# The last K part of a down projection in three column groups, with the final norm beside it

## The chip, the core and the metric

The kernel runs on one core of a Trainium2 chip. The metric is the device time of one execution in microseconds (us). TensorE (PE in the profile) multiplies; VectorE (DVE), ScalarE (ACT) and GpSimd (POOL) work on the elements; SyncE (SP), ACT and POOL start DMA transfers. Each engine runs its own instructions in the order in which they stand, and semaphores hold an instruction until what it needs is there.

## What is computed

A decoder layer over 528 positions (16 meta tokens and 512 tokens) of width 1024. Only its end matters here: a gated MLP whose down projection is added to the residual `h`, and a final RMSNorm over the 1024 channels.

```python
hn = rmsnorm(h, norm2_g[l])
up = causal_dwconv(hn @ w_up[l], conv_w[l], conv_b[l])
a, bv = jnp.split(up, 2, axis=-1)
h = h + (jax.nn.silu(a) * bv) @ w_down[l]      # K = 2816, N = 1024
return rmsnorm(h, final_norm_g)[:, N_META:]    # over the 1024 channels of each token
```

## The kernel before, in words

Channels lie on the 128 partitions and tokens along the free axis, so an activation of 1024 channels is 8 chunks of 128 x 528. Two neighbouring chunks share a tile: `h2.pair(i)` holds chunks 2i and 2i+1. All products are made to nearly full fp32 precision from rounded operands (type `F32R`): weights and activations are each split into a high and a low part (`split`, L270 to L272: ACT copies to the high part, DVE subtracts for the low one), and three products, high by high, high by low and low by high, are added up in PSUM. A matmul whose operands are plain `F32` is one instruction in the program and two records in the profile.

The tail of the program is a list `seq` of jobs (22 jobs "up", and the down projection in between and behind). The down projection's K of 22 blocks of 128 is cut into `PARTS` of 6, 6, 6 and 4 blocks; each part goes over the 8 output chunks in 4 jobs of two chunks (`c` = 0, 1). Part 0 and 1 stand among the "up" jobs, part 2 behind them, and part 3, the last four jobs (`base` = `len(seq) - 4`), has its own code, which is where the change is. `down` (L970 to L978) makes the products of one output chunk with one part: per block of K three matmuls against 128 x 128 weights, so 12 in part 3.

Part 3 before (L1003 to L1039): chunks 0 to 6 are each made over all 512 tokens at once (12 matmuls of 512 columns), DVE adds the sum to `h` (L1014), ACT squares it (L1019) and multiplies `h` by the norm's gain (`gf`, L1021), and the squares are added up in `tot3`, on POOL for four chunks and on DVE for two (L1020). Chunk 7 is made in two halves of 256 tokens. For each half, `ones32` (all ones, plain `F32`) times `tot3` and times the last chunk's squares gives the sum over the 1024 channels on every partition (L1026 and L1030), `rsqrt_mean` turns it into 1/root (ACT: Ln, L254, and Exp, L256; DVE: three steps that sharpen it, L258 to L260), and four multiplications of two chunks each (three on DVE, one on POOL, L1038) are followed by four output DMAs (L1039).

Weights of a down job arrive in a tile of the pool `rawp` (3 buffers, `fetch`, L574 for these jobs) over SP's queue and are split into two tiles of `gp` (2 buffers for high, 2 for low). So the split for a job waits until the products of the job two before it are done. The pool `ssp` (2 buffers of 1024 columns for high, 2 for low) holds block sums for the "up" jobs and is unused in parts 2 and 3. PSUM has 8 banks of 512 columns (`bank`), taken in turn.

The tile framework orders instructions of each engine when it builds the program. What ends up in which order is shown below where it matters.

Of the kernel before, what the change touches and what calls it, by code (L numbers as in the profile page):

```python
# [14 lines left out]
AF = mybir.ActivationFunctionType  # L15
ALU = mybir.AluOpType

P = 128
L = 528
META = 16  # L20
T0 = 14
TW = L - T0
D = 1024
# [17 lines left out]
CROSS = {(0, 1): 0, (1, 0): 1, (1, 1): 2, (2, 0): 3}  # L41
CROSS_X = {(0, 0): 0, (0, 1): 1, (1, 0): 2, (1, 1): 3}
PARTS = ((0, 6), (6, 6), (12, 6), (18, 4))
SUPERS = [(0, 16)] + [(16 + 128 * i, 128) for i in range(4)]

VEC = {}
# [26 lines left out]
def f32(ap):  # L73
    return ap.bitcast(F32)
# [3 lines left out]
def hybrid_block(ctx: ExitStack, tc: tile.TileContext, xt, g1d, wts, wsq, wdown, wglr, wgk, vecs, out):  # L78
    nc = tc.nc
    act, dve, pool, pe, sp = nc.scalar, nc.vector, nc.gpsimd, nc.tensor, nc.sync  # L80
# [46 lines left out]
    def big(name, dt=F32, home=None):  # L127
        return Pairs(name, home or HOME.get(name, firstp), dt)
# [4 lines left out]
    def ps(name):  # L133
        return psum.tile([P, 2, 512], F32, tag="ps", name=name)
# [42 lines left out]
    def project(name, j, xh, xl, cols, hook=None, ahead=PREP_AHEAD):  # L177
        hi, lo = chunk(j, ahead)
        acc = ps(name)
        products(acc, [(hi[:, k], lo[:, k], xh[k], xl[k]) for k in range(KT)], cols, hook=hook)  # L180
        return acc
# [13 lines left out]
    def parts_of(acc, cols):  # L195
        for s, (a, b) in enumerate(cols):
            yield (acc[s] if isinstance(acc, list) else acc[:, s])[:, : b - a], slice(a, b)
# [10 lines left out]
    def v1(name, i=0):  # L208
        c = VEC[name] + i
        return vec[:, c : c + 1]  # L210
# [16 lines left out]
    ones32 = const.tile([P, P], F32, tag="ones32", name="ones32")  # L227
# [24 lines left out]
    def rsqrt_mean(dst, acc, cols, n, tmp):  # L252
        for src, c in parts_of(acc, cols):
            act.activation(dst[:, c], src, AF.Ln, scale=1.0 / n, bias=eps_t)  # L254
        c = slice(cols[0][0], cols[-1][1])
        done = act.activation(dst[:, c], dst[:, c], AF.Exp, scale=-0.5)  # L256
        for src, h in parts_of(acc, cols):
            dve.scalar_tensor_tensor(tmp[:, h], src, n * EPS, dst[:, h], ALU.add, ALU.mult)  # L258
        dve.scalar_tensor_tensor(tmp[:, c], tmp[:, c], -0.5 / n, dst[:, c], ALU.mult, ALU.mult)
        last = dve.scalar_tensor_tensor(dst[:, c], tmp[:, c], 1.5, dst[:, c], ALU.add, ALU.mult)  # L260
        return done, last
# [8 lines left out]
    def split(hi, lo, src):  # L270
        act.activation(hi, src, AF.Copy)  # L271
        dve.tensor_tensor(lo, src, f32(hi), ALU.subtract)  # L272
# [11 lines left out]
    def scaled(dst, acc, cols):  # L284
# [9 lines left out]
        out=tri, in_=ones32, pattern=[[1, P]], base=0, channel_multiplier=-1,  # L294
# [32 lines left out]
    with tc.issue_after(ready[0].ins), tc.issue_after(ready[1].ins):  # L327
        for m in range(3):
            scaled(qk[4 + m], accs[m], FULL)
        acc = project("pk3", ORDER["k"] + 3, xh, xl, FULL)  # L330
# [7 lines left out]
    acc = ps("pglr")  # L338
# [35 lines left out]
    for i in range(2):  # L374
        two = slice(2 * i, 2 * i + 2)
# [12 lines left out]
    def head_decay(h):  # L388
# [3 lines left out]
        act.activation(q_far[:, T0:], b[:, T0:], AF.Exp, scale=-1.0 / TAU)  # L392
        for s, (t, n) in enumerate(SUPERS):
            if s:
# [12 lines left out]
    for m in range(8):  # L407
        acc = project(f"pv{m}", ORDER["v"] + m, xh, xl, FULL)
# [18 lines left out]
    def span(s):  # L427
        t, n = SUPERS[s]
        c = max(t, T0)
        return t, c, t + n - c  # L430
# [80 lines left out]
    for s in range(4):  # L511
        gla_back(s)
        gla_front(s + 1)
        hl = squares(s)
# [3 lines left out]
    hl = squares(4)  # L518
# [27 lines left out]
    def bank(name):  # L546
        return bankp.tile([P, 512], F32, tag="bank", name=name)

    between = {9: (0, 0), 10: (0, 2), 15: (1, 0), 16: (1, 2)}
    seq = [("plain", "u", 0)] + [("plain", "a", i) for i in range(3)]  # L550
# [5 lines left out]
    for i in range(FF):  # L556
        seq.append(("plain" if i < PLAIN else "fast", "up", i))
        if i in between:
            part, m = between[i]
            seq += [("down", part, m), ("down", part, m + 1)]  # L560
    seq += [("down", part, m) for part in (2, 3) for m in range(4)]
    loaded, own, sums = {}, {}, {}

    def fetch(n):
        if n >= len(seq) or n in loaded:
            return
        job = seq[n]
        t = rawp.tile([P, 4, 512], F32, tag="raw", name=f"raw{n}")
        if job[0] != "down":
            sp.dma_start(t, wsq[UNIT[job[1]] + job[2]])  # L570
        else:
            nk = PARTS[job[1]][1]
            flat_t = t.rearrange("p a b -> p (a b)")
            sp.dma_start(flat_t[:, 0 : 2 * nk * P], wdown[4 * job[1] + job[2], :, 0 : 2 * nk * P])  # L574
        loaded[n] = t

    def blocks(t):
        return t.rearrange("p a (k n) -> p a k n", n=P)
# [3 lines left out]
    def direct_tiles(n):  # L582
        if n not in own:
            fetch(n)
            job = seq[n]
            hl = [gp.tile([P, 3, 512], F32R, tag=f"g{c}", name=f"g{c}{n}") for c in "hl"]
            if job[0] == "down":
                k = 2 * PARTS[job[1]][1] * P
                hl = [t.rearrange("p a b -> p (a b)")[:, 0:k] for t in hl]
                own[n] = [t.rearrange("p (c k n) -> p c k n", c=2, n=P) for t in hl], hl, k  # L590
            else:
                own[n] = [blocks(t) for t in hl], hl, None
        return own[n]

    def split_here(n):
        return seq[n][0] == "down" or seq[n][1] in ("grp", "b", "o")
# [11 lines left out]
    def make_high(n):  # L608
        if n >= len(seq) or n in high_made:
            return  # L610
        high_made.add(n)
        _, (hi, lo), k = direct_tiles(n)
        if k is None:
            act.activation(hi, loaded[n][:, 0:3], AF.Copy)  # L614
            if split_here(n):
                dve.tensor_tensor(lo, loaded[n][:, 0:3], f32(hi), ALU.subtract)
        else:
            split(hi, lo, loaded[n].rearrange("p a b -> p (a b)")[:, 0:k])

    def two(name):  # L620
        return tuple(ssp.tile([P, 2, 4, P], F32R, tag=f"s{c}", name=f"s{c}_{name}") for c in "hl")
# [16 lines left out]
    def weights(n):  # L638
        make_low(n)
        make_high(n)  # L640
        make_sums(n)
        return (own[n][0], *sums.get(n, ()))
# [7 lines left out]
    def prepare(n, ins=None):  # L650
        fetch(n + 2)
        fetch(n + 3)
        behind(ins, make_low, n + 2)
# [4 lines left out]
    def pairtile(name, dt=F32):  # L658
        return flat(name, unitp, dt)
# [210 lines left out]
    for n in range(len(seq)):  # L870
        kind, name, i = seq[n]
# [16 lines left out]
        elif name == "ga":  # L888
            z, _ = unit_gate(n, i, name)
# [8 lines left out]
        elif name == "b":  # L898
            plain(n, i, pbh, pbl, TAIL, take_b)
            if i == 3:  # L900
                h2, h2h, h2l = big("h2", F32, unitp), big("h2h", F32R, lastp), big("h2l", F32R, lastp)
# [68 lines left out]
    def down(acc, w, c, part, cols):  # L970
        a, b = cols
        k0, nk = PARTS[part]
        for k in range(nk):
            for e, (p, q) in enumerate(((0, 0), (0, 1), (1, 0))):
                pe.matmul(  # L975
                    acc, w[p][:, c, k], gated[k0 + k][q][:, a:b],
                    start=k == 0 and e == 0, stop=k == nk - 1 and e == 2,
                )  # L978

    for n, job in enumerate(seq):  # L980
        if job[0] != "down" and job[1] != "up":
            continue
        if job[0] != "down":
            i = job[2]
# [7 lines left out]
        elif job[1] < 3:  # L992
# [3 lines left out]
            for c in range(2):  # L996
                acc = bank(f"pd{n}_{c}")
                down(acc, w, c, job[1], (0, 512))
                h = h2[2 * job[2] + c][:, META:]
                dve.tensor_tensor(h, acc, h, ALU.add)  # L1000
            prepare(n)

    sq3 = pairtile("sq3")  # L1003
    tot3, last3 = sq3[:, 0:512], sq3[:, 512:1024]
    base = len(seq) - 4
    for m in range(7):
        (w,) = weights(base + m // 2)
        make_high(base + m // 2 + 1)
        if m % 2:
            prepare(base + m // 2)  # L1010
        acc = bank(f"pe{m}")
        down(acc, w, m % 2, 3, (0, 512))
        h = h2[m][:, META:]
        dve.tensor_tensor(h, acc, h, ALU.add)  # L1014
        if m == 0:
            act.activation(tot3, h, AF.Square)
        else:
            sq = pairtile(f"n3_sq{m}")[:, 0:512]
            act.activation(sq, h, AF.Square)  # L1019
            (pool if m < 5 else dve).tensor_tensor(tot3, tot3, sq, ALU.add)  # L1020
        act.activation(h, h, AF.Copy, scale=v1("gf", m))  # L1021
    (w,) = weights(base + 3)
    for a, b in ((0, 256), (256, 512)):
        acc, s3 = bank(f"pd7_{a}"), bank(f"n3s_{a}")
        down(acc[:, 0:256], w, 1, 3, (a, b))
        pe.matmul(s3[:, 0:256], ones32, tot3[:, a:b], start=True, stop=False)  # L1026
        t = h2[7][:, META + a : META + b]
        dve.tensor_tensor(t, acc[:, 0:256], t, ALU.add)
        act.activation(last3[:, a:b], t, AF.Square)
        pe.matmul(s3[:, 0:256], ones32, last3[:, a:b], start=False, stop=True)  # L1030
        r3 = pairtile(f"r3_{a}")
        rstd3 = r3[:, 0:256]
        rsqrt_mean(rstd3, [s3], ((0, 256),), D, r3[:, 512:768])
        dve.tensor_scalar(t, t, v1("gf", 7), None, ALU.mult)
        wide = rstd3.unsqueeze(1).to_broadcast([P, 2, 256])
        for eng, q, i in ((dve, sp, 1), (pool, act, 0), (dve, sp, 2), (dve, act, 3)):
            y = h2.pair(i)[:, :, META + a : META + b]
            eng.tensor_tensor(y, y, wide, ALU.mult)  # L1038
            q.dma_start(out[2 * i : 2 * i + 2, :, a:b].rearrange("m p t -> p m t"), y)  # L1039


# [79 lines left out]
```

## Time and profile before

| | us |
|---|---|
| three runs, median (lowest to highest) | 833.92 (832.73 to 834.35) |
| the profiled execution | 836.4 |
| its span, from the first to the last instruction | 834.7 |
| chain that ended last: share of PE / DMA / DVE / ACT | 85% / 6% / 3% / 3% |
| first product of part 3 begins, from the span's start | 797.61 |
| last product of part 3 begins | 821.63 |

A run is timed without the profiler; the profiled execution is one more, 2.5 us above the median of the three. In the profile a row of the timeline has: start, time from the first record's start to the last one's end, engine, line, operation, tiles written and read, shape, and how many records were merged into the row. PEld is TensorE's loading of weights, which lies beside the products; PEclk is the clock that was granted to TensorE.

### The profile page before, as it was taken

What the parts mean: (1) busy time and instruction counts of PE and PEld (TensorE: products, weight loads), DVE (VectorE), ACT (ScalarE), POOL (GpSimd) and SP (SyncE); (2) the same over time, 40 slices, a digit from 0 to 9 for tenths busy, and PEclk for the clock granted to TensorE, in tenths of its full rate; (3) what the DMA queues carried; (4) which work ended last, traced back from release to release, by engine and by line L of the source; (5) the groups of instructions that cost most, each with busy time, mean ns of one, the idle gap of its engine ahead of it and who ended that gap; (6) DMA issues with size and microseconds to landing.
All of it is one profiled execution on the core that took longest, in us unless ns stands there. A gap on an engine that the chain in (4) does not pass through costs nothing.

```text
span 834.7 us, 14943 instructions
## 1 busy us (share of the span) xinstructions
PE 813.1 (97%) x6219; PEld 783.2 (94%) x6219; DVE 593.8 (71%) x887; ACT 477.9 (57%) x679; POOL 128.9 (15%) x153
## 2 busy tenths in 40 slices
PE   8999999999999999999999999999999999999994
PEld 6999999999999999999999999999989988999883
DVE  6668346779756797755564597998759965899845
ACT  7287244576655676644234457774557734786542
POOL 4000000011222122110003322220122110320021
PEclk9999999999999999999999999999999999999998
DMA  6413320158667778734342756875557644775102
GB/s 218 157 57 99 99 76 27 51 147 254 164 130 171 176 177 177 192 88 152 112 150 99 171 122 149 180 150 158 146 140 163 159 113 152 168 166 134 54 23 101
DMA packets 35572, 113.16 MB, mean 136 GB/s; under 512 B 3920, under 2 KB 6736, under 8 KB 29488
## 3 DMA queue, kind: packets, MB, share of 16 engines
q1 hardware_dynamic: 17856, 81.26, 29.4%
q0 software_dynamic: 16416, 29.89, 22.1%
q8 instruction: 48, 0.79, 0.4%
q10 hardware_dynamic: 1232, 1.05, 0.4%
q14 instruction: 20, 0.16, 0.1%
HBM read 110.10 MB, written 2.10 MB: 134 GB/s over the span
## 4 chain that ended last, share of the span: by engine, by line
PE 85%; DMA 6%; DVE 3%; ACT 3%; issue 1%; POOL 1%; SPq 0%; DVEq 0%; ACTq 0%
PE pp L672 18%; PE x L706 14%; PE pd L975 12%; PE q L706 9%; PE pv L172 6%; DMA gl<-in_wsq_dram 5%; PE y L706 5%; PE v L706 5%; PE pr L172 4%; PE pq L172 3%; PE pe L975 2%; PE pk L172 2%; PE pgrp L834 1%; PE po L472 1%; ACT gl L604 1%
## 5 line engine op out<-in xcount | busy, mean ns | idle before, releaser
L606 POOL DMA_DIRECT2D gl<-in_wsq_dram x114 | 102.0, 1207 | 500.3 <-ACT gl L604 421.9
L614 ACT ACTIVATE gh<-raw 128x1536 fp32r<-128x1536 f32 x47 | 69.9, 1486 | 61.0 <-PE pp L672 26.7
L633 DVE TENSOR_TENSOR raw<-raw 128x512 f32<-128x512 f32 x116 | 79.9, 689 | 26.7 <-ACT gh L614 14.3
L975 PE MATMUL pd<-g,gh 128*128 128x512 f32 (+1 forms) x304 | 93.3, 389 | 0.0
L975 PEld LDWEIGHTS pd<-g,gh 128*128 128x128 f32 x304 | 56.5, 188 | 12.3
L604 ACT ACTIVATE gl<-raw 128x1536 fp32r<-128x1536 f32 x38 | 56.2, 1478 | 9.3 <-issue 4.4
L975 PE MATMUL pd<-g,gl 128*128 128x512 f32 (+1 forms) x152 | 59.0, 388 | 0.0
L155 ACT ACTIVATE whi<-wraw 128x1024 fp32r<-128x1024 f32 (+2 forms) x28 | 25.9, 933 | 53.3 <-PE pv L172 25.8
L156 DVE TENSOR_TENSOR wlo<-wraw,whi 128x1024 fp32r<-128x1024 f32 (+2 forms) x28 | 30.6, 1100 | 7.0 <-ACT whi L155 5.8
L975 PEld LDWEIGHTS pd<-g,gl 128*128 128x128 f32 x152 | 28.6, 188 | 6.1
L960 ACT ACTIVATE cv<-z,vec 128x512 f32<-128x512 f32 x44 | 33.9, 813 | 0.0
L1000 DVE TENSOR_TENSOR h<-pd,h 128x512 f32<-128x512 f32 x24 | 16.5, 689 | 24.4 <-PE pd L975 24.3
L961 DVE SCALAR_TENSOR_TENSOR cv<-z,vec,cv 128x512 f32<-128x512 f32 x44 | 32.2, 746 | 0.0
L962 DVE SCALAR_TENSOR_TENSOR cv<-z,vec,cv 128x512 f32<-128x512 f32 x44 | 32.2, 746 | 0.0
L272 DVE TENSOR_TENSOR gl<-raw,gh 128x1536 fp32r<-128x1536 f32 (+1 forms) x16 | 26.0, 1624 | 6.4 <-ACT gh L271 6.4
L271 ACT ACTIVATE gh<-raw 128x1536 fp32r<-128x1536 f32 (+1 forms) x16 | 22.0, 1377 | 11.8 <-PE pd L975 9.1
L172 PE MATMUL pv<-xh,whi 128*128 128x264 f32 x128 | 26.4, 287 | 0.0
L172 PE MATMUL pr<-xh,whi 128*128 128x258 f32 (+1 forms) x128 | 25.9, 284 | 0.0
L172 PE MATMUL pv<-xl,whi 128*128 128x264 f32 x128 | 25.9, 283 | 0.0
L172 PE MATMUL pv<-xh,wlo 128*128 128x264 f32 x128 | 25.9, 283 | 0.0
L172 PE MATMUL pr<-xh,wlo 128*128 128x258 f32 (+1 forms) x128 | 25.8, 284 | 0.0
L172 PE MATMUL pr<-xl,whi 128*128 128x258 f32 (+1 forms) x128 | 25.6, 281 | 0.0
(1280 smaller groups left out, 2949.6 us busy)
## 6 DMA issues: line engine op xcount, KB each, us to landing
raw<-in_wsq_dram SPq DMA_DIRECT2D x47, 1024.0 KB, 5.7
gl<-in_wsq_dram POOLq DMA_DIRECT2D x114, 256.0 KB, 7.3
wraw<-in_wts_dram SPq DMA_DIRECT2D x22, 512.0 KB, 3.6
raw<-in_wdown_dram SPq DMA_DIRECT2D x12, 768.0 KB, 4.3
xb<-in_xt_dram SPq DMA_DIRECT2D x4, 528.0 KB, 5.4
h<-in_xt_dram SPq DMA_DIRECT2D x4, 514.0 KB, 5.3
raw<-in_wdown_dram SPq DMA_DIRECT2D x4, 512.0 KB, 3.5
x<-in_xt_dram SPq DMA_DIRECT2D x7, 264.0 KB, 6.2
```

The source lines that it names most:

```text
L156: dve.tensor_tensor(lo[:, a:b], t[:, a:b], f32(hi[:, a:b]), ALU.subtract)
L172: pe.matmul(acc[:, s, : b - a], w, x[:, a:b], start=(i == 0 and w is wh and x is xh), stop=(i == n - 1 and last),)
L604: act.activation(lo, loaded[n][:, 0:3], AF.Copy, scale=-1.0)
L606: pool.dma_start(lo[:, b], wsq[UNIT[name] + i, :, b], accum_op=ALU.add)
L614: act.activation(hi, loaded[n][:, 0:3], AF.Copy)
L633: dve.tensor_tensor(raw[:, dst], raw[:, dst], raw[:, x], ALU.add)
L672: pe.matmul(acc[:, 0 : b - a], w[p], q[k][:, a:b], start=k == 0 and e == 0, stop=k == KT - 1 and e == 2,)
L706: pe.matmul(acc[:, 0:n], w[a][:, block, k], x[k][b][:, at], start=first and k == 0 and e == 0, stop=k == 3 and e == 2, skip_group_check=no ...
L960: act.activation(cv, z[:, c, META:], AF.Identity, scale=v1("cw2", m), bias=v1("cb", m))
L961: dve.scalar_tensor_tensor(cv, z[:, c, META - 1 : L - 1], v1("cw1", m), cv, ALU.mult, ALU.add)
L962: dve.scalar_tensor_tensor(cv, z[:, c, META - 2 : L - 2], v1("cw0", m), cv, ALU.mult, ALU.add)
L975: pe.matmul(acc, w[p][:, c, k], gated[k0 + k][q][:, a:b], start=k == 0 and e == 0, stop=k == nk - 1 and e == 2,)
```

## The change

Part 3 goes over the tokens in three groups, `CUTS` of 224, 160 and 128 columns, and within each group over all four pairs of output chunks. So the weights of all four jobs are needed at once: jobs `base` and `base + 1` keep their tiles in `gp`, the last two are given those of `ssp`, and all four are fetched and split ahead of the first group. The two chunks of a pair lie side by side in one PSUM bank, so DVE's addition, ACT's square and DVE's sum of squares take both at once; POOL has no work left there. `finish` is the norm of a group: four sums on PE over the two halves of `tot` and of the last pair's squares, `rsqrt_mean`, four multiplications on DVE and four output DMAs. For the first two groups it is written behind the second pair's products of the next group; for the last group it stands alone. There ACT's queue takes two of the four DMAs, otherwise SP's takes all.

```diff
+CUTS = ((0, 224), (224, 384), (384, 512))
...
             job = seq[n]
+            if n >= len(seq) - 2:
+                hl = two(f"{n}")
+                own[n] = hl, [t.rearrange("p a k n -> p (a k n)") for t in hl], 1024
+                return own[n]
             hl = [gp.tile([P, 3, 512], F32R, tag=f"g{c}", name=f"g{c}{n}") for c in "hl"]
...
-    sq3 = pairtile("sq3")
-    tot3, last3 = sq3[:, 0:512], sq3[:, 512:1024]
     base = len(seq) - 4
-    for m in range(7):
-        (w,) = weights(base + m // 2)
-        make_high(base + m // 2 + 1)
-        if m % 2:
-            prepare(base + m // 2)
-        acc = bank(f"pe{m}")
-        down(acc, w, m % 2, 3, (0, 512))
-        h = h2[m][:, META:]
-        dve.tensor_tensor(h, acc, h, ALU.add)
-        if m == 0:
-            act.activation(tot3, h, AF.Square)
-        else:
-            sq = pairtile(f"n3_sq{m}")[:, 0:512]
-            act.activation(sq, h, AF.Square)
-            (pool if m < 5 else dve).tensor_tensor(tot3, tot3, sq, ALU.add)
-        act.activation(h, h, AF.Copy, scale=v1("gf", m))
-    (w,) = weights(base + 3)
-    for a, b in ((0, 256), (256, 512)):
-        acc, s3 = bank(f"pd7_{a}"), bank(f"n3s_{a}")
-        down(acc[:, 0:256], w, 1, 3, (a, b))
-        pe.matmul(s3[:, 0:256], ones32, tot3[:, a:b], start=True, stop=False)
-        t = h2[7][:, META + a : META + b]
-        dve.tensor_tensor(t, acc[:, 0:256], t, ALU.add)
-        act.activation(last3[:, a:b], t, AF.Square)
-        pe.matmul(s3[:, 0:256], ones32, last3[:, a:b], start=False, stop=True)
-        r3 = pairtile(f"r3_{a}")
-        rstd3 = r3[:, 0:256]
-        rsqrt_mean(rstd3, [s3], ((0, 256),), D, r3[:, 512:768])
-        dve.tensor_scalar(t, t, v1("gf", 7), None, ALU.mult)
-        wide = rstd3.unsqueeze(1).to_broadcast([P, 2, 256])
-        for eng, q, i in ((dve, sp, 1), (pool, act, 0), (dve, sp, 2), (dve, act, 3)):
-            y = h2.pair(i)[:, :, META + a : META + b]
-            eng.tensor_tensor(y, y, wide, ALU.mult)
-            q.dma_start(out[2 * i : 2 * i + 2, :, a:b].rearrange("m p t -> p m t"), y)
+    for i in range(4):
+        fetch(base + i)
+        make_high(base + i)
+
+    def finish(part, a, b, tot, last):
+        w = b - a
+        s3 = bank(f"n3s_{part}")
+        for e, x in enumerate((tot[:, 0], tot[:, 1], last[:, 0], last[:, 1])):
+            pe.matmul(s3[:, 0:w], ones32, x, start=e == 0, stop=e == 3)
+        r3 = pairtile(f"r3_{part}")
+        rstd3 = r3[:, 0:w]
+        rsqrt_mean(rstd3, [s3], ((0, w),), D, r3[:, 512 : 512 + w])
+        wide = rstd3.unsqueeze(1).to_broadcast([P, 2, w])
+        for i in range(4):
+            y = h2.pair(i)[:, :, META + a : META + b]
+            dve.tensor_tensor(y, y, wide, ALU.mult)
+            (act if part == len(CUTS) - 1 and i % 2 else sp).dma_start(
+                out[2 * i : 2 * i + 2, :, a:b].rearrange("m p t -> p m t"), y
+            )
+
+    late = None
+    for part, (a, b) in enumerate(CUTS):
+        w = b - a
+        tot = None
+        for i in range(4):
+            wt = own[base + i][0]
+            acc = bank(f"pe{part}_{i}")
+            both = acc[:, 0 : 2 * w].rearrange("p (c n) -> p c n", c=2)
+            for c in range(2):
+                down(both[:, c], wt, c, 3, (a, b))
+            if i == 1 and late:
+                finish(*late)
+            h = h2.pair(i)[:, :, META + a : META + b]
+            dve.tensor_tensor(h, both, h, ALU.add)
+            sq = pairtile(f"n3_sq{part}_{i}")[:, 0 : 2 * w].rearrange("p (c n) -> p c n", c=2)
+            act.activation(sq, h, AF.Square)
+            if tot is None:
+                tot = sq
+            elif i < 3:
+                dve.tensor_tensor(tot, tot, sq, ALU.add)
+            for c in range(2):
+                if part == len(CUTS) - 1 and i == 3:
+                    dve.tensor_scalar(h[:, c], h[:, c], v1("gf", 2 * i + c), None, ALU.mult)
+                else:
+                    act.activation(h[:, c], h[:, c], AF.Copy, scale=v1("gf", 2 * i + c))
+        late = part, a, b, tot, sq
+    finish(*late)
```

Three places in the built programs show what that moves. The first is PE, in the middle of the second group (lines of the changed kernel lie 5 higher up to L1000). `pe_1_9034` and `pe_2_9084` are the products of the second and third pair, `n3s_9059` the sum of squares of the first group; `g_...` are the activations' halves, `gh`/`gl` and `sh`/`sl` the weights' high and low parts.

```order
L980 MATMUL pe_1_9034<-g_8680,gh_8868 128x160 x2
L980 MATMUL pe_1_9034<-g_8680,gl_8869 128x160
L1017 MATMUL n3s_9059<-n_sq_0_8908,ones_126 128x224 x2
L1017 MATMUL n3s_9059<-n_sq_3_9000,ones_126 128x224 x2
L980 MATMUL pe_2_9084<-g_8644,sh_8872 128x160 x2
L980 MATMUL pe_2_9084<-g_8644,sl_8873 128x160
```

PE before, in the last chunk's second half (`pd_256_9040`), with the first half's sums (`n3s_9008`) among its products and the second half's behind them:

```order
L1026 MATMUL n3s_9008<-sq_8868,ones_126 128x256
L975 MATMUL pd_256_9040<-g_8644,gh_8949 128x256 x2
L975 MATMUL pd_256_9040<-g_8644,gl_8950 128x256
L975 MATMUL pd_256_9040<-g_8656,gh_8949 128x256
L1030 MATMUL n3s_9008<-sq_8868,ones_126 128x256
L975 MATMUL pd_256_9040<-g_8656,gh_8949 128x256
```

The sums of a group are now four instructions in one place, with 48 products of the next group ahead of them; before they were two, one of them behind 4 products. The second place is DVE around the start of part 3, where the low parts of the weights are made (`raw_8820` is job `base + 1`, `raw_8866` and `raw_8876` the last two). Before:

```order
L272 TENSOR_TENSOR gl_8823<-raw_8774,gh_8822 128x1024
L1000 TENSOR_TENSOR h_4877<-pd_0_8826,h_4877 128x512
L1000 TENSOR_TENSOR h_4877<-pd_1_8846,h_4877 128x512
L272 TENSOR_TENSOR gl_8870<-raw_8820,gh_8869 128x1024
L1014 TENSOR_TENSOR h_4868<-pe_8873,h_4868 128x512
```

And now:

```order
L273 TENSOR_TENSOR gl_8823<-raw_8774,gh_8822 128x1024
L273 TENSOR_TENSOR sl_8873<-raw_8866,sh_8872 128x1024
L1005 TENSOR_TENSOR h_4877<-pd_0_8826,h_4877 128x512
L273 TENSOR_TENSOR sl_8879<-raw_8876,sh_8878 128x1024
L1005 TENSOR_TENSOR h_4877<-pd_1_8846,h_4877 128x512
L273 TENSOR_TENSOR gl_8869<-raw_8820,gh_8868 128x1024
L1042 TENSOR_TENSOR h_4868<-pe_0_8882,h_4868 128x2x224
```

The splits for the last two jobs have moved ahead, into the time of part 2; the one for `base + 1` is still behind them. The third place is DVE's end in the changed program, from the second group's norm (`r_1_9205`) to the last group's (`r_2_9291`):

```order
L261 SCALAR_TENSOR_TENSOR r_1_9205<-r_1_9205 128x160
L1024 TENSOR_TENSOR h_4868<-h_4868,r_1_9205 128x2x160
L1024 TENSOR_TENSOR h_4871<-h_4871,r_1_9205 128x2x160
L1024 TENSOR_TENSOR h_4874<-h_4874,r_1_9205 128x2x160
L1024 TENSOR_TENSOR h_4877<-h_4877,r_1_9205 128x2x160
L1042 TENSOR_TENSOR h_4874<-pe_2_9225,h_4874 128x2x128
L1048 TENSOR_TENSOR n_sq_0_9171<-n_sq_0_9171,n_sq_2_9251 128x256
L1042 TENSOR_TENSOR h_4877<-pe_3_9256,h_4877 128x2x128
L1051 TENSOR_SCALAR h_4877<-h_4877,vec 128x128 x2
L259 SCALAR_TENSOR_TENSOR r_2_9291<-n3s_9286,r_2_9291 128x128
```

The second group's four multiplications stand ahead of the last group's third and fourth additions, and behind the last addition only the last group's own norm is left; before, the first half's multiplications stood between the last addition and the second half's norm.

## The prediction

> **What bounds the kernel now.** I read the engines' totals first, then the chain of work that ended last, then the windows of the stage that changes, then single rows of its end.
>
> ```profile
> span 834.7 us, 14943 instructions
> PE 813.1 (97%) x6219; PEld 783.2 (94%) x6219; DVE 593.8 (71%) x887; ACT 477.9 (57%) x679; POOL 128.9 (15%) x153
> ...
> 797.77 19.37 PE pe L975 x84
> 817.14 0.02 issue
> 817.16 0.70 DVE h L1014
> ...
> 797.61:821.63 24.02, 23.21 (x113) 19.32 (x111) 11.29 (x15) 13.54 (x20) 6.07 (x4) 1.00 0.00 0
> 821.63:834.70 13.07, 1.42 (x7) 0.61 (x5) 8.79 (x14) 1.60 (x4) 3.07 (x2) 0.71 0.47 161
> ```
>
> The first row pair says that PE is the bound nearly everywhere, and that weight loads (PEld) are as many as matmuls: each matmul brings its own load, even where two in a row use the same weights. The chain says the same of part 3. The windows cut its end in two: from the first product's start to the last product's start 24.02 us, in which PE is busy for 23.21, and then 13.07 us in which PE does next to nothing and the norm, the multiplications and the output run one behind the other. The change wants to shorten the second stretch; I ask what it costs in the first. All durations are of the profiled execution (span 834.7 us, 836.4 in all). Its span is 0.8 us above the median of the runs, 833.92; the change of the span is carried over to that median.
>
> **What a product costs, by its width.**
>
> ```profile
> 797.61 0.62 PE L975 MATMUL pe<-g,gh 128*128 128x512 f32 x2
> ...
> 816.96 0.40 PE L975 MATMUL pd<-g,gh 128*128 128x256 f32 x2
> ...
> 818.27 0.28 PE L975 MATMUL pd<-g,gl 128*128 128x256 f32 x1
> ...
> 118.32 1.87 PEld L472 LDWEIGHTS po<-att,vnat 128*128 128x128 f32 x16
> ...
> 118.44 1.84 PE L472 MATMUL po<-att,vnat 128*128 128x2 f32 x16
> ...
> 129.75 0.39 PE L471 MATMUL po<-kq_far,state 128*128 128x128 f32 x2
> ...
> 131.31 0.39 PE L472 MATMUL po<-att,vnat 128*128 128x128 f32 x2
> ...
> 127.97 0.19 PEld L500 LDWEIGHTS nos<-osh,ones 128*128 128x128 f32 x1
> 128.09 0.19 PEld L500 LDWEIGHTS nos<-osl,ones 128*128 128x128 f32 x1
> 128.20 0.19 PEld L463 LDWEIGHTS pst<-vn_h,kn 128*128 128x128 f32 x1
> ```
>
> A row's length holds overlap; what counts is the distance from start to start. 84 products of 512 columns take 816.96 - 797.61 = 19.35 us, 0.230 each. The next 12, of 256 columns, start 0.119 apart (818.27 is the twelfth: 1.31 / 11). Half the columns, half the time, so down to 256 the columns set the pace. Below that the trace shows something else. In the chunked attention 16 records of only 2 columns follow each other, and their loads take 1.87 us, of which the last one's own 0.19 is taken off: 1.68 / 15 = 0.112. At 128 columns the distance is the same, (131.31 - 129.75) / 14 = 0.1114. **A fresh 128 x 128 weight tile costs about 0.111 us, however few columns follow.** Those are plain F32 records; the only narrow ones of the type that part 3 uses (F32R, written `nos`, 8 columns) have loads 0.12 and 0.11 apart, so the floor is there too. By the two rows of 256 and 2 columns a width between them costs between 0.112 and 0.119; I take 0.1114 for all three, the load being the later of the two at 224 columns already (on the line through 512 and 256 columns that width would stream in 0.105).
>
> The Trainium skill (TensorE: Matmul & The Clock Gate, section "LDWEIGHTS (loading the stationary operand)") gives a load P / 1.2 ns for P columns, 107 ns here. It speaks against this change as the rows do, and the trace's 111 lies close; with 107 the forecast below would be an estimate of 838.9.
>
> **The sum, first stretch.** Before, part 3 has 7 x 12 products of 512 columns and 2 x 12 of 256: 108 weight loads. Now each group loads all weights again: 3 groups x 8 chunks x 12 = 288 products, 96 at each width. From the first product's start to the last one's: 287 x 0.1114 = 31.97 us.
>
> The norm's sums of the first two groups stand among the products, four plain F32 matmuls each, so eight records.
>
> ```profile
> 820.37 0.59 PE L1030 MATMUL n3s<-sq,ones 128*128 128x256 f32 x2
> ...
> L1030 PE MATMUL n3s<-sq,ones 128*128 128x256 f32 x2 | 0.6, 377 | 0.0
> ```
>
> At 256 columns the second record starts 0.59 - 0.377 = 0.213 behind the first; at 128 it is 0.111 (above); between them 0.188 at 224 and 0.137 at 160. 8 x 0.188 + 8 x 0.137 = 2.60 us. Their inputs are long there: 48 products, over 5 us, lie between a group's last product and its sums, and an addition and a square take some 1.3 us. So the stretch is 31.97 + 2.60 = **34.57 against 24.02: +10.55 us**.
>
> Two waits could come on top. The weights of the second pair are needed at the 27th product instead of the 51st, at 797.61 + 26 x 0.1114 = 800.51.
>
> ```profile
> 798.72 1.23 DVE L272 TENSOR_TENSOR gl<-raw,gh 128x1024 fp32r<-128x1024 f32 x1 [0.22 <-ACT gh L271]
> ```
>
> They are ready at 799.95, held by the `gp` buffer that part 2 frees; the other two splits are ahead of it, in DVE's idle time of part 2. 0.56 us of cover remain, so this costs nothing; without the cover it costs what is late, one to one. On DVE the second group's multiplications lie ahead of the last group's third and fourth additions. By my clock the sums end at 827.1 (797.61 + 240 x 0.1114 + 2.60 is 826.95, and the pipeline), Ln, a square, Exp and a sum of squares bring 828.5, three steps and four multiplications 831.3, the third addition, its square and sum 832.6, just when the last products end. I take 0 and keep 0.5 us for it. The output DMAs of the first two groups, eight on SP's queue, end microseconds ahead; nothing but the last group's stands behind them.
>
> **The sum, last stretch.** The rows of before, of 256 columns, and what they become at 128 (two chunks at once make 256 again in DVE's additions and multiplications and ACT's square):
>
> ```profile
> 821.63 0.28 PE L975 MATMUL pd<-g,gl 128*128 128x256 f32 x1
> ...
> 822.30 0.42 DVE L1028 TENSOR_TENSOR h<-pd,h 128x256 f32<-128x256 f32 x1
> 822.63 0.42 DVE L259 SCALAR_TENSOR_TENSOR r<-r 128x256 f32<-128x256 f32 x1
> 822.75 0.42 ACT L1029 ACTIVATE sq<-h 128x256 f32<-128x256 f32 x1 [0.82 <-DVE h L1028]
> ...
> 823.22 0.70 PE L1030 MATMUL n3s<-sq,ones 128*128 128x256 f32 x2 [0.87 <-ACT sq L1029]
> ...
> 823.68 2.95 DVE L1038 TENSOR_TENSOR h<-h,r 128x512 f32<-128x512 f32 x3
> 823.95 0.47 ACT L254 ACTIVATE r<-n3s,eps_t 128x256 f32<-128x256 f32 x1 [0.79 <-PE n3s L1030]
> ...
> 825.36 0.42 ACT L256 ACTIVATE r<-r 128x256 f32<-128x256 f32 x1 [0.93 <-POOL h L1038]
> ...
> 826.56 0.41 DVE L258 SCALAR_TENSOR_TENSOR r<-n3s,r 128x256 f32<-128x256 f32 x1
> ...
> 827.93 2.96 DVE L1038 TENSOR_TENSOR h<-h,r 128x512 f32<-128x512 f32 x3
> ...
> L1019 ACT ACTIVATE n_sq<-h 128x512 f32<-128x512 f32 x6 | 3.8, 630 | 5.5 <-DVE h L1014 5.5
> L1014 DVE TENSOR_TENSOR h<-pe,h 128x512 f32<-128x512 f32 x7 | 4.8, 692 | 8.8 <-PE pe L975 8.8
> ...
> DMA to landing us min/median/max: 2.1/2.4/3.2
> ```
>
> From 512 to 256 columns ACT gains 0.63 - 0.42 = 0.21 and DVE 0.69 - 0.42 = 0.27, so to 128 half of that, 0.11 and 0.14. Behind the last product's start: the product 0.28; addition 0.04 + 0.42; square 0.03 + 0.42; the last two sums, four records of 128 instead of two of 256, as long as those, 0.05 + 0.70; Ln 0.04 + 0.36; Exp 0.03 + 0.31; three DVE steps, before (827.93 - 826.56) = 1.37, now 0.97, and 0.03 ahead; four multiplications of 256, 0.33 apart (822.30 to 822.63), 3 x 0.33 + 0.42 = 1.41; and from the last one's end to the span's end as before, 834.70 - (827.93 + 2.96) = 3.81. The sum is **8.90 against 13.07: -4.17 us**. What goes is the wait of Exp behind POOL's multiplication (0.93) and of the second half's steps behind the first half's multiplications (823.68 to 826.56), and shorter operations. The last DMAs are half as large but rows of 512 bytes; none like it is in the trace, so I bound the 3.81 by the landings, 0.3 less to 0.8 more.
>
> Net: 10.55 - 4.17 = +6.4 us. The span goes to 841.1, the profiled execution to 842.8, and 833.92 to **840.3 us**.
>
> **The rivals.**
>
> *The load hides (not slower).* If F32R weights load faster than plain ones, the columns alone set the pace: 0.105, 0.077 and 0.063 on the line through 512 and 256 columns, 96 x 0.245 = 23.5, and 23.5 + 2.6 - 24.0 - 4.2 = -2.1: 831.8. It decides where a load costs under some 0.09 us: there 288 x 0.09 = 25.9, and the gain in the last stretch pays for it. Against it: the two 8-column loads at 0.12 and 0.11, and loads of 0.19 each for both types. For it: no F32R row between 8 and 256 columns. The Trainium skill (the same page, section "Weight-path perf modes — Fast Weight Load (FWL) and DoubleRow") has a quick load, on for 128 weights of a type that is not FP32, which says neither yes nor no for F32R; no run here shows it. Chance 0.06.
>
> *Narrow F32R runs like plain F32.* Nothing in the trace excludes it. A plain matmul takes two records: 0.376, 0.274 and 0.223 at the three widths, 96 x 0.873 = 83.8, so 52 us more: 892. For: before keeps every F32R product at 256 columns or over but for the one pair. Against: each of that pair has one load, as the wide ones have. Chance 0.08.
>
> *DVE is late for the last group*, by more than the 0.5 above, or the weights of the second pair are: 1 to 3 us more, 841.3 to 843.3. The margin at the end is about nothing. Chance 0.14.
>
> **How the numbers follow.** The forecast has 0.72. Its own ends: 287 x (0.119 - 0.1114) = 2.2 more if the 256-column distance holds, 287 x 0.003 = 0.9 less if a load is a little quicker, -0.3 and +0.8 for the output, 0.5 for DVE, and the runs spread by -1.2 and +0.4. That and the third rival give 837.8 to 844.3; the first two rivals, 0.14 together, stay out. Faster by over 0.2% (1.7 us, about what a measurement of this kernel can tell from no change): 0.03, half of the first rival, whose time lies at that edge; within it 0.05; slower 0.92.
>
> **What would show it.** Right: the products of part 3 start 0.11 apart in all three groups, PEld is busy without a gap there, the stretch from first to last product is 34 to 36 us, and about 9 us lie behind it. Wrong: a distance that falls with the width (first rival), one twice or three times as large (second), or PE rows with idle time ahead of `pe` or `n3s` that DVE released (third).

## The result and the profile after

| | before | after |
|---|---|---|
| median of 6 runs, us (lowest to highest) | 834.44 (832.73 to 835.28) | 840.61 (838.84 to 841.80) |
| profiled execution, its span | 834.7 | 839.4 |

The change makes the kernel slower. The medians differ by 6.2 us; the ratio of the runs, which is not the quotient of the two medians, is 1.0066 with a 95% interval of 1.0046 to 1.0085, that is 5.5 us (3.8 to 7.1). The forecast was 840.3.

The two windows of the prediction, in the changed kernel: from the first product's start of part 3 to the last one's, and from there to the end. Columns as before: length, then busy time of PE, PEld, DVE, ACT and POOL, the granted clock, the DMA share and GB/s.

```profile
796.48:831.07 34.59, 34.59 (x304) 34.59 (x303) 16.59 (x34) 15.43 (x37) 0.00 (x0) 1.00 0.12 39
831.07:839.37 8.30, 1.69 (x11) 1.18 (x10) 3.42 (x11) 1.57 (x5) 0.00 (x0) 0.80 0.32 96
```

The first stretch went from 24.02 to 34.59 us, 10.57 more; the second from 13.07 to 8.30, 4.77 less. PEld is now busy in every moment of the first stretch (34.59 of 34.59); it was so for 19.32 of 24.02 before. A load's record is 0.19 us long, so PEld reads as busy at any distance below that; the distances further down say more. The span grew by 4.7 only, since in this execution part 3 began 1.1 us earlier (796.48 against 797.61). The code ahead of it is the same but for the fetch and the split of the last two jobs' weights, which have moved into it, and in the runs below the start of part 3 lies anywhere from 794.6 to 799.7, with either order of the code: the stretches are to be compared, or medians, not single spans.

The timeline of the changed kernel's PE, at the beginning, where the second group begins, and at the end of the products (start, length, records merged):

```profile
796.48 0.37 PE L980 MATMUL pe<-g,gh 128*128 128x224 f32 x2
...
807.19 0.36 PE L980 MATMUL pe<-g,gh 128*128 128x160 f32 x2
...
812.52 1.71 PE L1017 MATMUL n3s<-n_sq,ones 128*128 128x224 f32 x8
813.91 0.51 PE L980 MATMUL pe<-g,sh 128*128 128x160 f32 x2
814.26 0.27 PE L980 MATMUL pe<-g,sl 128*128 128x160 f32 x1
...
830.86 0.38 PE L980 MATMUL pe<-g,sh 128*128 128x128 f32 x2
831.07 0.28 PE L980 MATMUL pe<-g,sl 128*128 128x128 f32 x1
```

96 products of 224 columns take 807.19 - 796.48 = 10.71 us, 0.1116 each. The 48 of 160 columns up to the first group's sums take 812.52 - 807.19 = 5.33, 0.1110 each. Thirty per cent fewer columns, the same time. From 812.52 to 814.26 the eight records of the first group's sums and the two products behind them take 1.74 us. (1.39 us lie between the start of the sums and that of the next product, but that product and the one behind it start some 0.23 us apart, so part of the sums' time shows only there.) Without two products at 0.111 the sums take 1.52.

And the end, on DVE, ACT and PE in order of time:

```profile
830.86 0.43 DVE L1048 TENSOR_TENSOR n_sq<-n_sq,n_sq 128x256 f32<-128x256 f32 x1 [0.48 <-ACT n_sq L1044]
...
831.39 0.42 DVE L1042 TENSOR_TENSOR h<-pe,h 128x256 f32<-128x256 f32 x1
831.85 0.42 ACT L1044 ACTIVATE n_sq<-h 128x256 f32<-128x256 f32 x1 [0.29 <-DVE h L1042]
...
832.31 0.71 PE L1017 MATMUL n3s<-n_sq,ones 128*128 128x128 f32 x4 [0.27 <-ACT n_sq L1044]
833.06 0.37 ACT L255 ACTIVATE r<-n3s,eps_t 128x128 f32<-128x128 f32 x1 [0.80 <-PE n3s L1017]
833.46 0.31 ACT L257 ACTIVATE r<-r 128x128 f32<-128x128 f32 x1
833.80 0.29 DVE L259 SCALAR_TENSOR_TENSOR r<-n3s,r 128x128 f32<-128x128 f32 x1 [1.03 <-ACT r L257]
...
834.78 1.43 DVE L1024 TENSOR_TENSOR h<-h,r 128x256 f32<-128x256 f32 x4
```

Each step of the chain follows the one before it within 0.05 us: 0.98 us for the three steps of the norm, 1.43 for the four multiplications, which end at 836.21, and 3.16 from there to the end of the span.

### The profile page after: what moved, and what is told of

It is laid out like the page before. It is cut to its first block, busy times and chain, and to the rows that moved or that the text cites. A ratio compares the mean times of both kernels' runs of the same rounds, so it can differ in the third digit from the quotient of the medians.

```text
span 839.4 us, 15370 instructions
## 1 busy us (share of the span) xinstructions
PE 825.7 (98%) x6415; PEld 799.2 (95%) x6415; DVE 595.7 (71%) x903; ACT 481.9 (57%) x699; POOL 118.4 (14%) x147
## 4 chain that ended last, share of the span: by engine, by line
PE 90%; DMA 4%; ACT 3%; DVE 1%; issue 1%; POOL 1%; SPq 0%; DVEq 0%; ACTq 0%
PE pp L677 21%; PE x L711 13%; PE pd L980 12%; PE q L711 9%; PE pv L173 6%; PE pr L173 5%; PE y L711 5%; PE v L711 4%; PE pe L980 4%; DMA gl<-in_wsq_dram 4%; PE pq L173 3%; PE pgrp L839 1%; PE pk L173 1%; PE po L473 1%; ACT gl L609 1%
## 5 line engine op out<-in xcount | busy, mean ns | idle before, releaser
L980 PE MATMUL pd<-g,gh 128*128 128x512 f32 x288 | 89.8, 393 | 0.0
L980 PEld LDWEIGHTS pd<-g,gh 128*128 128x128 f32 x288 | 53.8, 188 | 12.2
L980 PE MATMUL pd<-g,gl 128*128 128x512 f32 x144 | 56.7, 394 | 0.0
L273 DVE TENSOR_TENSOR gl<-raw,gh 128x1536 fp32r<-128x1536 f32 (+1 forms) x14 | 23.5, 1678 | 5.9 <-ACT gh L272 5.9
L272 ACT ACTIVATE gh<-raw 128x1536 fp32r<-128x1536 f32 (+1 forms) x14 | 19.9, 1420 | 4.5 <-PE pd L980 2.7
```

Of the source, the lines that this page charges most:

```text
L980: pe.matmul(acc, w[p][:, c, k], gated[k0 + k][q][:, a:b], start=k == 0 and e == 0, stop=k == nk - 1 and e == 2,)
```

## The experiments

The theory: a product costs the longer of its columns and its weight load, and the load, 0.111 us, is the longer one at all three widths; the change makes 288 loads out of 108. The rivals were that the cost comes with the groups (waits, sums, DVE's queue), and that narrow products are dear, or cheap, by their columns. Medians below stand beside runs of the kernel before on the same chip.

**1. The loads without the groups.** In the kernel before, each product of 512 columns of part 3 is made as three.

```diff
-        down(acc, w, m % 2, 3, (0, 512))
+        for a, b in ((0, 224), (224, 384), (384, 512)):
+            down(acc[:, a:b], w, m % 2, 3, (a, b))
```

> The kernel before, in which each product of 512 columns in the last part is made as three of 224, 160 and 128: the weight loads of the change without its groups, its sums or its norm. Load theory: 252 products 0.1116 apart instead of 84 at 0.2304, 28.1 us instead of 19.35: 8.8 us more, first to last product 32.8 instead of 24.0, the last stretch as before at 13.1: 843.2. Rival (the change's cost lies in its groups, sums and waits, not in loads): 834 to 835.

Measured: 843.24 (842.21 to 844.23, 4 runs) beside 834.24, ratio 1.0109, interval 1.0092 to 1.0126. The windows of this kernel:

```profile
794.74:827.55 32.81, 31.94 (x280) 31.66 (x279) 11.29 (x15) 13.45 (x20) 6.08 (x4) 1.00 0.00 1
827.55:840.62 13.07, 1.41 (x7) 0.61 (x5) 8.80 (x14) 1.60 (x4) 3.07 (x2) 0.75 0.47 161
```

32.81 against the 32.8 expected, and a last stretch of 13.07 as in before. The same columns, sums and norm with 168 more products, each with its load, cost 9 us. This alone is more than the whole change lost.

**2. Two groups, and four.** Only the table of cuts is changed.

```diff
-CUTS = ((0, 224), (224, 384), (384, 512))
+CUTS = ((0, 256), (256, 512))
```

> The change with two groups of 256 columns instead of 224, 160 and 128. Load theory (each product costs the later of its weight load, 0.112 us, and its columns, 0.119 us at 256): 192 products instead of 288, first product to last product 191 x 0.119 + 8 x 0.213 = 24.4 us instead of the 34.5 measured with three groups; the stretch behind it grows from 8.3 to about 10.9, since every step of the norm is twice as wide. 833.1 us, 7.5 under the change and 1 under before. Rival (the cost lies in the groups, in waits and sums, some 5.2 us for each group beyond the first): 29.3 us from first to last product, 838.

and with `CUTS = ((0, 128), (128, 256), (256, 384), (384, 512))`:

> The change with four groups of 128 columns. Load theory: 384 products 0.1116 apart and three sums of eight records 0.111 apart, 42.7 + 2.7 = 45.4 us from first to last product instead of 34.5, the last stretch stays at 8.3: 851.5 us. Rival (some 5.2 us for each group): 39.7 us, 845.8.

Measured: with two groups 834.75 (12 runs) beside 834.41, ratio 1.0001 (0.9987 to 1.0015); with four 851.07 in one run. The windows, two groups first and four groups behind:

```profile
795.19:819.62 24.43, 24.43 (x201) 24.22 (x199) 11.73 (x19) 12.40 (x24) 0.00 (x0) 1.00 0.01 3
819.62:832.03 12.41, 2.51 (x11) 1.42 (x9) 6.20 (x13) 1.52 (x3) 0.00 (x0) 0.83 0.48 165
```

```profile
795.43:840.83 45.40, 45.40 (x409) 45.39 (x407) 18.17 (x46) 18.77 (x52) 0.00 (x0) 1.00 0.12 33
840.83:849.36 8.53, 1.48 (x11) 1.10 (x10) 3.21 (x10) 1.09 (x3) 0.00 (x0) 0.78 0.26 77
```

The first stretches are 24.4 and 45.4, as the loads give them; 5.2 us for each group, the rival, would be 29.3 and 39.7 and is out. The last stretch of two groups missed: 12.41 instead of 10.9, and with it the time, forecast at 833.1. DVE's timeline of that kernel shows 0.85 us of it:

```profile
818.94 1.29 DVE L1024 TENSOR_TENSOR h<-h,r 128x512 f32<-128x512 f32 x2
820.14 0.68 DVE L1048 TENSOR_TENSOR n_sq<-n_sq,n_sq 128x512 f32<-128x512 f32 x1
820.75 0.68 DVE L1042 TENSOR_TENSOR h<-pe,h 128x512 f32<-128x512 f32 x1
```

The last product starts at 819.62 and is done 0.28 later, but the addition that takes it up starts at 820.75: the first group's multiplications (L1024) and a sum of squares are ahead of it on DVE. This is the prediction's third rival, in a kernel where the group is wide enough. Most of the rest is the output of 256 columns: from the last multiplication's end to the span's end it is 3.88 us here, against 3.16 in the change.

**3. Fewer columns, as many loads.** `down` in the changed kernel runs ten of its twelve products over fewer columns, 32, 64 or 128 (`n` below), and leaves that part of the sums out.

```diff
+                ends = part < 3 or (k, e) in ((0, 0), (nk - 1, 2))
+                n = b - a if ends else 32
                 pe.matmul(
-                    acc, w[p][:, c, k], gated[k0 + k][q][:, a:b],
+                    acc[:, 0:n], w[p][:, c, k], gated[k0 + k][q][:, a : a + n],
```

> The change, but of the twelve products of each chunk and group only the first and the last run over all columns of the group, the ten between them over 32 columns, so most of that part of the down projection is left out. Weight loads are as many as in the change. Load theory: the products stay 0.111 apart, first to last product 34 to 34.5 us, 840.6 us give or take the spread. Rival (the narrow products cost by their columns, whatever the reason): 240 of 288 products fall to 0.06 us or less, 12 us or more less, 828 or below.

> The change, but of the twelve products of each chunk in the groups of 224 and 160 columns only the first and the last run over all columns, the ten between them over 128; the left-out columns make the output differ. As many weight loads, a third fewer columns. Load theory: 34.5 us from first to last product as in the change, products 0.111 to 0.112 apart, and a granted clock of 1.00. Rival (columns set the pace at these widths): on the line through 512 and 256 columns 80 products gain 0.042 and 80 gain 0.014: 4.5 us less, 30.

> As the run with 32 columns, with 64: ten of twelve products of each chunk and group run over 64 columns, the other two over all; most of that part is left out. With 32 columns the granted clock fell to 0.5 some 2.5 us into the part and every product then took 0.213 us; with 128 it stayed at 1.00. If the clock follows how much of the time columns stream (82 columns a product on average here, 64 with 32, 101 to 144 in the run with 128 and the change) this one may lie on either side: products 0.111 apart and 840, or 0.21 apart and some 865. In no case does the distance fall under 0.111; if it does, the load theory is wrong.

Measured, one run each: 867.71 with 32 columns, 866.04 with 64, 839.65 with 128. With 128 the first stretch is 34.59 us, the change's to the hundredth, at a granted clock of 1.00:

```profile
795.06:829.65 34.59, 34.59 (x304) 34.59 (x303) 16.64 (x34) 15.42 (x37) 0.00 (x0) 1.00 0.12 39
```

With 32 the kernel is 27 us slower than the change, which neither theory nor rival had expected. The windows of that kernel, three early stretches of part 3 (the eighth column is the granted clock), and PE's timeline before and after:

```profile
796.00:799.00 3.00, 3.00 (x29) 3.00 (x27) 2.25 (x4) 1.06 (x1) 0.00 (x0) 1.00 0.00 0
799.00:802.00 3.00, 3.00 (x16) 3.00 (x16) 0.49 (x1) 1.43 (x3) 0.00 (x0) 0.51 0.00 0
802.00:830.00 28.00, 28.00 (x141) 27.78 (x142) 6.20 (x13) 7.23 (x17) 0.00 (x0) 0.56 0.00 1
```

```profile
797.47 0.26 PE L982 MATMUL pe<-g,gl 128*128 128x32 f32 x1
797.58 0.37 PE L982 MATMUL pe<-g,gh 128*128 128x32 f32 x2
797.81 0.26 PE L982 MATMUL pe<-g,gl 128*128 128x32 f32 x1
797.92 0.37 PE L982 MATMUL pe<-g,gh 128*128 128x32 f32 x2
798.14 0.26 PE L982 MATMUL pe<-g,gl 128*128 128x32 f32 x1
```

```profile
804.77 0.37 PE L982 MATMUL pe<-g,sh 128*128 128x32 f32 x1
804.99 0.37 PE L982 MATMUL pe<-g,sl 128*128 128x32 f32 x1
805.20 0.59 PE L982 MATMUL pe<-g,sh 128*128 128x32 f32 x2
```

While the clock is full the products of 32 columns start (798.14 - 797.47) / 6 = 0.112 us apart, the floor for this type of operand, seen directly. Then the clock halves and they start 0.21 apart. So the expectation of an unchanged time was wrong, for the clock, and there is a floor at both clocks; products that cost by their columns would have gone far below 0.111. With 64 columns the distance is 0.111 before the clock falls (nine products from 797.07 to 798.07) and 0.21 behind it. (The averages in the last expectation are partly off: over all three groups they are 55 columns with 32, 82 with 64, 128 to 144 a group with 128 and 128 to 224 in the change.)

Is the floor the load, or a fixed cost of a product? Each product here has its own load, so their numbers can't tell. Rows of the same kernel can, where a chunk ends and the next begins, each with a product of 224 columns; PE first, PEld behind:

```profile
798.48 0.35 PE L982 MATMUL pe<-g,gl 128*128 128x224 f32 x1
798.66 0.30 PE L982 MATMUL pe<-g,gh 128*128 128x224 f32 x2
798.81 0.26 PE L982 MATMUL pe<-g,gl 128*128 128x32 f32 x1
```

```profile
798.45 0.19 PEld L982 LDWEIGHTS pe<-g,gl 128*128 128x128 f32 x1
798.56 0.30 PEld L982 LDWEIGHTS pe<-g,gh 128*128 128x128 f32 x2
798.78 0.19 PEld L982 LDWEIGHTS pe<-g,gl 128*128 128x128 f32 x1
```

The row of two at 798.66 holds a product of 224 columns and one of 32. It ends at 798.96, and a product of 32 columns is 0.26 long, so the second one starts at about 798.70: 0.18 and then 0.04 us lie between three products. Their loads start at 798.45, 798.56, 798.67 (the row's end less 0.19) and 798.78, 0.11 apart throughout. So two products can start closer than 0.111, and the loads keep the even pace: these rows speak for the load. A kernel with products that share one load was not run.

**4. The last stretch of before.** The norm's multiplications that POOL had are given to DVE, and with them the first half's outputs go to SP's queue.

```diff
-        for eng, q, i in ((dve, sp, 1), (pool, act, 0), (dve, sp, 2), (dve, act, 3)):
+        for eng, q, i in ((dve, sp, 1), (dve, sp, 0), (dve, sp, 2), (dve, act if a else sp, 3)):
```

> The kernel before with the two multiplications of the norm that POOL does given to DVE, and the first half's outputs all on SP's queue. The step on trial is that Exp of the second half waits 0.93 us behind ACT's DMA start for POOL's result, and that DVE's multiplications beside POOL's take 1.75 us instead of 0.68. Theory: both go, DVE gets two more of 0.60; from 823.68 to the last multiplication's end 6.4 us instead of 7.2: 0.8 us less, 833.6. Rival (DVE's long multiplications have another cause): they stay at 1.75 and the two more make it 0.4 to 1.2 slower.

Measured: 833.55 (12 runs) beside 834.41, ratio 0.9989 (0.9974 to 1.0005), which doesn't clear the spread. In the traces the last stretch is 12.17 us (822.23 to 834.40) instead of 13.07, which the kernel before and the one of experiment 1 both have, Exp no longer waits, and four multiplications on DVE alone take less than three beside POOL's:

```profile
824.28 2.49 DVE L1038 TENSOR_TENSOR h<-h,r 128x512 f32<-128x512 f32 x4
826.69 0.41 DVE L258 SCALAR_TENSOR_TENSOR r<-n3s,r 128x256 f32<-128x256 f32 x1
...
828.06 2.50 DVE L1038 TENSOR_TENSOR h<-h,r 128x512 f32<-128x512 f32 x4
```

Before, the first of these rows was 2.95 for three, the longest of them 1.75. The gain is DVE's, and not Exp's. In the kernel before, the chain that ended last goes from the multiplications to the norm's next step without Exp:

```profile
823.77 2.87 DVE h L1038 x3
826.64 0.35 DVE r L258
```

Exp had ended at 825.36 + 0.42 = 825.78, 0.78 us before that step began (826.56), so its wait of 0.93 lay beside DVE's work and cost nothing. The first half's multiplications went from 2.88 us (823.68 to 826.56) to 2.41 (824.28 to 826.69), the second half's from 2.96 to 2.50: 0.93 together. That POOL's work and not the outputs' other queue made the difference was not tried apart. So 0.9 of the 4.8 us that the change gained at the end needed no groups at all.

**5. Towards a version that beats both.** Two groups of 256 columns (`CUTS` as in experiment 2), with the first group's norm behind the first pair of the second group:

```diff
-            if i == 1 and late:
+            if i == 0 and late:
```

> Two groups of 256 columns, and the first group's norm written behind the first pair of the second group's products instead of the second pair. In the run with two groups the last addition started 0.85 us late, behind the first group's multiplications on DVE. Theory (DVE's queue was what made the last stretch 12.4 us instead of 11): first to last product 24.4 us as there, the last stretch 11.5: 35.9 us instead of 37.1 in before, 833.2. Rival (the last stretch is long for its wide steps alone): 12.4 us again, no gain on before.

Measured: 833.70 (11 runs) beside 834.24, ratio 0.9987 (0.9972 to 1.0001). Its last stretch is 11.65 us and the first 24.39: 0.76 of the 12.41 was DVE's queue, and the last addition is now late by 0.10 instead of 0.85. Then with one sum fewer on PE (`tot`'s two halves are added on DVE, so three sums are left):

```diff
-        for e, x in enumerate((tot[:, 0], tot[:, 1], last[:, 0], last[:, 1])):
-            pe.matmul(s3[:, 0:w], ones32, x, start=e == 0, stop=e == 3)
+        for e, x in enumerate((tot[:, 0], last[:, 0], last[:, 1])):
+            pe.matmul(s3[:, 0:w], ones32, x, start=e == 0, stop=e == 2)
...
+                if i == 2:
+                    dve.tensor_tensor(tot[:, 0], tot[:, 0], tot[:, 1], ALU.add)
```

> As the run with two groups and the early norm, and DVE adds the two halves of the sums of squares, so that PE makes three sums for a group instead of four: two records of 0.213 us less between the first group's products and 0.42 us more on DVE where it waits anyway. Theory: first to last product 24.0 us, the last stretch 11.5, 35.5 us instead of 37.1: 832.8. Rival (DVE is full): the last stretch grows by the 0.4 saved.

Measured: 833.77 beside 834.24, ratio 1.0000 (0.9983 to 1.0018). The first stretch fell to 23.96 as expected and the last grew to 12.11, as the rival said: DVE gave the 0.4 back. Last, the early norm with the final multiplication and DMA cut by chunk:

```diff
+            if part == len(CUTS) - 1 and i == 3:
+                for c in range(2):
+                    dve.tensor_tensor(y[:, c], y[:, c], rstd3, ALU.mult)
+                    (act if c else sp).dma_start(out[6 + c, :, a:b], y[:, c])
+                continue
```

> Two groups of 256 columns with the early norm, and the very last multiplication and output cut by chunk, so that the last DMA carries 128 KB instead of 256. In the change, whose last DMAs carry 128 KB, 3.16 us lie between the last multiplication's end and the span's end; in before, with 256 KB, 3.81. Theory (the size of the last transfer makes that difference): first to last product 24.4 us, the last stretch 11.64 - 0.5 = 11.1; 1.6 us under before, 832.7. Rival (a DMA's start and landing make it up, whatever its size): 11.6 to 11.8, 833.3.

Measured: 834.50 beside 834.51, ratio 0.9982 (0.9962 to 1.0003), and a last stretch of 11.65: the rival. The transfers of the last group, in the DMA view of that kernel from 828 to 835.7 us (40 slices of 0.19 us) and of the change from 834 to 839.4 (40 of 0.135), say what a smaller last DMA doesn't change:

```profile
DMA  0000000000000003999999999999999300000000
GB/s 0 0 0 0 0 0 0 0 0 0 0 0 0 0 0 128 356 298 367 351 325 367 383 373 351 340 346 335 346 335 351 96 0 0 0 0 0 0 0 0
DMA packets 1104, 1.05 MB, mean 136 GB/s; under 512 B 80, under 2 KB 1104, under 8 KB 1104
```

```profile
DMA  0000000000000000799999999899930000000000
...
DMA packets 1088, 0.52 MB, mean 97 GB/s; under 512 B 64, under 2 KB 1088, under 8 KB 1088
```

The 1.05 MB of a group of 256 columns keep the DMA engines over 90% busy for some 3 us without a gap, at about 350 GB/s; the last piece waits behind the others. A group of 128 columns has half of it. From the last multiplication's end to the span's end it is 3.81 to 3.88 us in all seven traces that end on 256 columns, and 3.1 to 3.4 in all five that end on 128 (the change, four groups, and the three of experiment 3). No version beat the kernel before by more than its interval. By the stretches the three with the early norm come nearest, with 1 us less in both together (36.0 to 36.1 against 37.1), and the kernel of experiment 4, with no groups, has 36.2.

## Why the prediction was right, step by step

*The products.* 287 x 0.1114 us for the three widths was 31.97, and the sums 2.60: 34.57 for the first stretch. Measured 34.59, and the parts fit too: the first group's sums take 1.52, the second group's 1.09 (824.74 to 826.05 with two products), and these 2.61 leave 31.98 for the products. The floor, argued from rows of 2 and 128 columns of plain F32 and one pair of 8 columns of F32R, is now shown by the number of products alone (experiments 1 and 2) and by their indifference to the columns (3); that it is the load rests on the rows at the end of experiment 3. The Trainium skill (TensorE: Matmul & The Clock Gate, section "LDWEIGHTS (loading the stationary operand)") gives P / 1.2 ns for P columns; by that, 30.6 us would be the estimate for the products, where the trace has 32.0.

*The first rival, a load that hides,* is out by the same runs, and so is *the second, F32R at the price of plain F32*: 0.1116 at 224 columns, not 0.376.

*The waits.* The second pair's weights were in time: the products go on at 0.1116 throughout the first group. (The prediction has them needed at the 27th product "instead of the 51st". A pair has 24 products in both kernels, so it is the 27th in both; what changed is that 26 products take 2.9 us instead of 6.0. The cover of 0.56 us doesn't depend on that.) DVE's queue had been put at a margin of nothing, and it was: DVE was free at 830.86 + 0.43 = 831.29, the last product was done at 831.07 + 0.28 = 831.35, and the addition starts at 831.39. With wider groups it was late by 0.85, which is the third rival in another kernel.

*The last stretch* was put at 8.90 and came out at 8.30. Every step up to the last multiplication's end is within 0.02 us of its term, 0.05 too long in all; the mis-sized term is the output, 3.81 us from the last multiplication's end to the span's end, which measured 3.16 (836.21 to 839.37). I had carried the 3.81 over and bounded it by 0.3 less, as if it hung on a DMA's landing alone; it came out 0.65 less. The DMA views above show the queue of the whole group in it, 1.05 MB then and 0.52 MB now. The traces by width agree, and the size of the last piece alone changed nothing, but the bytes of a group were not varied by themselves.

*What went at the end.* The prediction names Exp's wait of 0.93 us behind POOL's multiplication. That wait was off the critical path and cost nothing; the 0.90 of experiment 4 is nearly the same number by chance, and is what DVE's multiplications gained without POOL's beside them. The sum didn't need this reading, since it was made of the steps that remain.

*The net* of +6.4 us is +6.2 by the medians, +5.5 by the ratio and 10.57 - 4.77 = +5.8 by the stretches: the direction and the mechanism were right, and 0.6 us of the end was not. That the median lies within 0.3 us of 840.3 is in part luck, since the six runs of the kernel before have a median 0.5 us above the three that the forecast started from.

## What to carry to other kernels

Where products are cut finer to let a tail begin earlier, count weight loads, not columns: find the width at which a product's distance stops falling in the trace (here 0.119 us at 256 columns, 0.111 at 224 and at 32), and cut to that width and no further. Here even that width gained 1 us by the stretches, and nothing clear of the spread by the medians. The tail that is to be hidden should first be looked at for what slows it by itself, since that may go without any cutting. And an engine that is lifted off the critical path by the regrouping, DVE here, has its queue filled in the place where the last group needs it.

## What was not expected of the hardware

TensorE's clock fell to half although the profile shows PE without an idle moment. With ten of twelve products at 32 or 64 columns, the granted clock went from 1.00 to about 0.5 some 3 us into the part and mostly stayed there (0.51, 0.56 and 0.50 in stretches of the run with 32; 0.54, 0.50 with 64), while the view has PE and PEld busy without a gap; with 128 columns and more it stayed at 1.00. Averaged over the twelve products of a chunk in the first group, where the clock fell, that is 64 columns ((10 x 32 + 2 x 224) / 12) and 91 in 0.111 us, against 144 with 128. That the share of time in which columns stream decides it fits all runs here, and was not tested by itself. The two runs have one more sign of it. Among products of 32 or 64 columns stand the first group's sums, eight records of 224 columns, and about their end the clock came back to 1.00 for a while and then fell again; the second group's sums, of 160 columns, didn't bring it back. By the granted clock in windows of 0.1 us it fell at 799.07, rose at 826.38 and fell at 829.79 with 32 columns, and at 799.26, 826.57 and 829.98 with 64: in both runs 3.41 us between the last two, and 27.31, eight times that, between the first two. So all six changes lie on a grid of 3.41 us. The floor under a product nearly doubled with the clock, from 0.112 to 0.21 us. The Trainium skill (TensorE: Matmul & The Clock Gate, section "Part 1: The HAM clock gate (the "warmup" mystery)") ties the half clock to an idle window of about 3.4 us; the time scale agrees (3.41), the idleness doesn't, unless waiting for weights counts as idle.
